# Half of a stage's input turned by a transposing DMA instead of by TensorE, at four places of a two-layer decoder trunk

## The chip, the cores and the metric

One core of a Trainium2 chip runs the whole program. The metric is the time of one execution on the device in microseconds, from the runtime's own start to its end; three runs of a kernel are shown by their median. A profiled execution has its own time, and a span, which goes from its first to its last instruction.

## The reference, cut to what matters

The input `x` has 256 tokens of 1024 numbers, all in fp32. The residual stream `h` runs through two layers; in each it passes three sub-layers (an FFN, a mixer, an FFN), every one with a norm before and behind it. The first layer's mixer is a gated linear recurrence (RG-LRU), the second's is attention on keys and values that are made from the stream between the two layers.

```python
for layer in range(2):
    if layer == 1:
        k, v, c = shared_kv(h, kv_norm_g, w_kv, w_fgate, b_fgate)
    f = swiglu(rms_norm(h, ffn1_pre_g[layer]), ffn1_w_gate[layer], ffn1_w_up[layer], ffn1_w_down[layer])
    h = h + 0.5 * rms_norm(f, ffn1_post_g[layer])
    hn = rms_norm(h, mix_pre_g[layer])
    m = recurrent_block(hn, ...) if layer == 0 else forgetting_attention(hn, ..., k, v, c)
    h = h + rms_norm(m, mix_post_g[layer])
    f = swiglu(rms_norm(h, ffn2_pre_g[layer]), ffn2_w_gate[layer], ffn2_w_up[layer], ffn2_w_down[layer])
    h = h + 0.5 * rms_norm(f, ffn2_post_g[layer])
```

So between the sub-layers `h` is normed and multiplied by the next weight matrix, which needs `h` with the features on the partitions, that is, transposed.

## The kernel before, in words

**Precision by three products.** TensorE multiplies in fp32r, and each fp32 operand is split in an upper part (a copy by ScalarE, called ACT below) and a lower part (the difference, by VectorE, DVE). A product is three matmuls: upper by upper, upper by lower, lower by upper. Weights are split like that as they come: `load_raw` (L161 and L164, a DMA of up to 512 KB on the queue of SP) fills one of five `raw` buffers, `split` makes `whi` (L173, ACT) and `wlo` (L177, DVE), of which there are nine each. One such unit of weights is an item: in most stages two k tiles (128 of the 1024 features each) by 512 columns.

**Two rows of tokens.** `h[0]` and `h[1]` are the tokens 0 to 127 and 128 to 255 (t=0 and t=1). Each item is multiplied first for t=0 and, some slots later, for t=1; `run` lets t=0 go 7 items ahead and then alternates. TensorE (PE) runs in exactly the order in which the program is written. The other engines' order is made by a scheduler at build time, by priorities (`tc.high_priority`) and, where `keep_in_program_order` stands, as written. Once built, each engine runs its own list in order and waits where an operand is not ready. `defer(n, f)` puts work n+1 slots later in the written order.

**From one sub-layer to the next.** `enter(t, ...)` is called when the last product of a sub-layer for row t is written. It takes sums of squares (ACT, into a tile `junk`), makes the scale on GpSimd (POOL) and adds the normed result to `h[t]` in two halves of 512 features (L297, DVE). A few slots later its inner function `inputs` prepares the next stage's operand: `to_tp` (L226) transposes `h[t]` on PE, four 128x128 tiles for each half, into a PSUM bank `gt`; `to_x` then multiplies each half by the gain (`xg`, L234, DVE, which also brings it to SBUF), copies it to the upper part `xhi` (L235, ACT) and takes the lower part `xlo` (L240, DVE). `stat` makes the scale of the norm, which is applied behind the product. At the layer's change there are two targets: `xhi`/`xlo` for the FFN and `zhi`/`zlo` for keys and values, with a gain of its own.

**Tiles that two uses share.** `t1` has two buffers of 512 columns, for products in `enter`, for `xg`, and for the halves in the next point. `junk` has one buffer.

**The other way to transpose, in use already.** The FFN's hidden values, keys, queries of t=1 and gates go another way: `planes` (POOL) parts each fp32 in two 16-bit planes, a transposing DMA on SP's queue turns both (`DMA_TRANSPOSE`, L535 for hidden values, L216 for the others, through `swap`), and `join` (POOL, L540 or L220) puts the halves together again. There are 56 such transfers.

The function `enter` is called for the output of the recurrence (rows go on to the FFN after it), for that of the attention, and for the four FFNs.

Of the kernel before, what the change touches and what calls it, by code (L numbers as in the profile page):

```python
# [9 lines left out]
F32 = mybir.dt.float32  # L10
# [33 lines left out]
def trunk_kernel(ctx: ExitStack, tc: tile.TileContext, A: dict, out: bass.AP):  # L44
# [13 lines left out]
    def nm(s):  # L58
        uid[0] += 1
        return f"{s}_{uid[0]}"  # L60
# [168 lines left out]
    def x_upper(tp, dest, n):  # L229

        gi, xh, xl = dest
        xg = hpool.tile([P, 4, P], F32, tag="t1", name=nm("xg"), bufs=2)
        g = gT[:, gi + 4 * n:gi + 4 * n + 4].unsqueeze(2).to_broadcast([P, 4, P])
        nc.vector.tensor_tensor(xg, tp.rearrange("p (a b) -> p a b", a=4), g, ALU.mult)  # L234
        nc.scalar.activation(xh[:, 4 * n:4 * n + 4, :], xg, AF.Copy)  # L235
        return xg

    def x_lower(xg, dest, n):
        gi, xh, xl = dest
        nc.vector.tensor_tensor(xl[:, 4 * n:4 * n + 4, :], xg, xh[:, 4 * n:4 * n + 4, :].bitcast(F32), ALU.subtract)  # L240

    def to_x(tps, dest):

        with tc.high_priority():
            xg = [x_upper(tps[n], dest, n) for n in range(2)]
            for n in range(2):
                x_lower(xg[n], dest, n)

    def to_x_tiles(tps, dest):

# [15 lines left out]
    def stat(t):  # L266
        ss = new_ss()
        square_sum(h[t], ss[:, 0:1])
        rs[t] = rstd_of(ss, 1)

    def enter(t, dests, pf, gb, half, last=False, normed=False, wait=3):

        f = 1.0 / 16 if half else 1.0 / 32
        ss = new_ss()
        t1 = []
        urgent = tc.high_priority()
        urgent.__enter__()
        for n in range(2):
            square_sum(pf[n], ss[:, n:n + 1], f)
        for n in range(2):  # L280
            if n == 1 and last:
                r = rstd_of(ss, 2, f, nc.vector)
            t1.append(hpool.tile([P, 512], F32, tag="t1", name=nm("t1"), bufs=2))
            nc.vector.tensor_tensor(t1[n], pf[n], gb[:, n * 512:(n + 1) * 512], ALU.mult)
        if not last:
            r = rstd_of(ss, 2, f)

        sp, aq = nc.sync, nc.scalar
        pieces = [(n * 512, 512, None) for n in range(2)]
        if last:  # L290
            pieces = ([(0, 1024, sp)] if t == 0 else
                      [(0, 256, sp), (256, 256, aq), (512, 256, sp), (768, 256, aq)])
        for c, m, q in pieces:
            hn = h[t][:, c:c + m]
            for a in range(c, c + m, 512):
                n = min(m, 512)
                nc.vector.scalar_tensor_tensor(h[t][:, a:a + n], t1[a // 512][:, a % 512:a % 512 + n], r[:, 0:1],  # L297
                                               h[t][:, a:a + n], ALU.mult, ALU.add)
            if last:
                q.dma_start(out[0, t * P:(t + 1) * P, c:c + m], hn)  # L300
        urgent.__exit__(None, None, None)
        if last:
            return

        def inputs():
            tps = [to_tp(h[t], n) for n in range(2)]
            for dest in dests:
                to_x(tps, dest)
            stat(t)

        def norm():
            with tc.high_priority():
                normed_x()

        def normed_x():
            ss = new_ss()
            for n in range(2):
                square_sum(h[t][:, n * 512:(n + 1) * 512], ss[:, n:n + 1])
            rs[t] = rstd_of(ss, 2)
            hn = []  # L320
            for n in range(2):
                hn.append(hpool.tile([P, 512], F32, tag="t1", name=nm("hn"), bufs=2))
                nc.vector.tensor_scalar(hn[n], h[t][:, n * 512:(n + 1) * 512], rs[t][:, 0:1], None, ALU.mult)

            def go():
                tps = []
                for n in range(2):
                    tp = gtbank()
                    for j in range(4):
                        nc.tensor.transpose(tp[:, j * P:(j + 1) * P], hn[n][:, j * P:(j + 1) * P], ident)  # L330
                    tps.append(tp)
                to_x_tiles(tps, dests[0])
            defer(6, go)

        if normed:
            norm()
            settled[0] = True
        else:
            defer(wait, inputs)
# [152 lines left out]
    def ahead(i, fn):  # L492
# [5 lines left out]
            return prep()  # L498
        items[i] = (both, work)

    def ffn_items(pool_of, wg, wu, wd, post_g, next_dests, last=False, normed=False):
        hid = {}
        sil = {}
        box = {}

        def hid_tiles(t):
            if t not in hid:
                hid[t] = (pool_of().tile([P, 22, P], F32R, tag=f"hhi{t}", name=nm("hhi"), bufs=1),
                          pool_of().tile([P, 22, P], F32R, tag=f"hlo{t}", name=nm("hlo"), bufs=1))
            return hid[t]  # L510

        def post_gate(c0, nn):
            def f(t, ps):
                s = pool_of().tile([P, 512], F32, tag="sil", name=nm("sil"), bufs=2)
                nc.scalar.activation(s[:, :nn], ps, AF.Silu, scale=rs[t][:, 0:1])  # L515
                sil[t] = s
            return f

        def post_up(c0, nn):
            def f(t, ps):  # L520
                hh, hl = hid_tiles(t)
                s = sil[t][:, :nn]
                pr = pool_of().tile([P, 512], F32, tag="prod", name=nm("prod"), bufs=2)
                nc.vector.scalar_tensor_tensor(pr[:, :nn], ps, rs[t][:, 0:1], s, ALU.mult, ALU.mult)  # L524
                halves = hpool.tile([P, 512], F32, tag="t1", name=nm("pl"), bufs=2).bitcast(U16)[:, :2 * nn]
                turned = pr.bitcast(U16)[:, :2 * nn].rearrange("p (a b) -> p a b", b=P)
                nc.gpsimd.tensor_copy(halves.rearrange("p (h f) -> p h f", h=2),  # L527
                                      pr[:, :nn].bitcast(U16).rearrange("p (f h) -> p h f", h=2))
                defer(2, lambda: hidden_T(halves, turned, hh, hl))

            def hidden_T(halves, turned, hh, hl):

                m, k0 = nn // P, c0 // P
                keep = tc.keep_in_program_order
                keep(nc.sync.dma_start(turned, halves, transpose=True))  # L535
                hv = hh[:, k0:k0 + m, :].rearrange("p a b -> p (a b)")
                lv = hl[:, k0:k0 + m, :].rearrange("p a b -> p (a b)")

                def join():
                    nc.gpsimd.tensor_copy(halves.rearrange("p (f h) -> p h f", h=2),  # L540
                                          turned.rearrange("p (h a) b -> p h (a b)", h=2))

                def parts():
                    x = halves.bitcast(F32)
                    keep(nc.scalar.activation(hv, x, AF.Copy))  # L545
                    keep(nc.vector.tensor_tensor(lv, x, hv.bitcast(F32), ALU.subtract))  # L546
                defer(3, join)
                defer(7, parts)
            return f

        i0 = len(items)
        for i in range(5):
            proj_items(wg, i * 512, 512, main_x, post_gate(i * 512, 512))
            proj_items(wu, i * 512, 512, main_x, post_up(i * 512, 512))

        last_up = post_up(2560, 256)

        def post_both(t, pg, pu):
            post_gate(2560, 256)(t, pg)
            last_up(t, pu)  # L560

        pair_items(wg, wu, 2560, 256, main_x, post_both)

        def load_gb():
            box["gb"] = gain_bcast(post_g)

        ahead(i0 + 24, load_gb)

        def post_down(t, accs):
            enter(t, next_dests(t), accs, box["gb"], True, last, normed)  # L570

        row_items(wd, [P] * 22, lambda t, k: (hid[t][0][:, k, :], hid[t][1][:, k, :]), post_down, 4 if last else 2)
        return i0

# [644 lines left out]
    def post_q(n):  # L1219
        return lambda t, ps: heads_T(ps, t, n, HD ** -0.5, att["q"][t])  # L1220

    for n in range(2):
        proj_items(A["attn_w_q"][0], n * 512, 512, main_x, post_q(n))
    n_q[0] = len(items)
    row_items(A["attn_w_o"][0], [P] * 8, lambda t, k: (att["oh"][t][:, k, :], att["ol"][t][:, k, :]),
              lambda t, accs: enter(t, [main_dest(GI[("ffn2", 1)], t)], accs, gbox["mix1"], False, wait=4),
              rows0=1, late=True)
    ahead(n_q[0] + 2, load_gb("mix1", A["mix_post_g"][1]))
    n_att = len(items)
# [240 lines left out]
```

## Time and profile before

| | |
|---|---|
| median of 3 runs | 966.11 us (965.6 to 966.61) |
| the profiled execution | 965.92 us |
| its span | 964.2 us |
| PE, PE's weight loads | 955.9 us busy (99%), 791.3 us (82%) |
| DVE, ACT, POOL | 640.7 us (66%), 527.6 us (55%), 218.2 us (23%) |
| granted TensorE clock | 0.999 |
| DMA | 198.79 MB, mean 206 GB/s |

A profile's row in order of time reads: start and duration in us (from the span's start), engine, line of the kernel, operation, what it writes and reads, how many instructions are merged in the row, and in brackets the idle time of the engine before it and what ended that. The chain of work that ended last goes back from the last instruction to what released it, and so on. In a view of one line the three numbers are the shortest, median and longest duration in ns.

### The profile page before, as it was taken

How to read it: one execution, taken by the hardware profiler on the slowest of the kernel's cores; microseconds unless marked ns; L12 is line 12 of the kernel's file. 1: busy time of each engine (PE TensorE's matmuls, PEld its weight loads, DVE VectorE, ACT ScalarE, POOL GpSimd, SP SyncE). 2: the span in 40 equal slices, each digit the busy share in tenths (PEclk: the TensorE clock that was granted, in tenths of full speed). 3: DMA queues.
4: the chain of work that ended last, by engine and by line, in shares of the span. 5: the costliest groups of instructions: out<-in, count | busy, mean ns of one | idle time of the engine just before them, and what ended most of it. 6: DMA issues, size and time to landing. Idle time of an engine off the chain costs nothing.

```text
span 964.2 us, 12866 instructions
## 1 busy us (share of the span) xinstructions
PE 955.9 (99%) x4575; PEld 791.3 (82%) x4575; DVE 640.7 (66%) x845; ACT 527.6 (55%) x750; POOL 218.2 (23%) x221
## 2 busy tenths in 40 slices
PE   9999999999999999999999999999999999999997
PEld 6888888898878888888898888888887788888886
DVE  6658674678997666664686566665488876666642
ACT  7546453568886555443565455444366855444431
POOL 2712330130001323230003522234022012232200
PEclk9999999999999999999999999999999999999999
DMA  8787995475346787775558979878773468777731
GB/s 286 226 258 225 256 284 197 142 228 163 119 123 219 209 236 211 205 242 196 135 182 278 253 219 258 230 216 265 226 256 97 133 199 236 207 222 233 223 109 44
DMA packets 148934, 198.79 MB, mean 206 GB/s; under 512 B 67166, under 2 KB 85958, under 8 KB 148742
## 3 DMA queue, kind: packets, MB, share of 16 engines
q1 hardware_dynamic: 146182, 191.06, 65.6%
q0 software_dynamic: 2080, 6.38, 2.1%
q8 instruction: 36, 0.59, 0.2%
q10 hardware_dynamic: 608, 0.53, 0.2%
q14 instruction: 28, 0.23, 0.1%
HBM read 182.19 MB, written 3.16 MB: 192 GB/s over the span
## 4 chain that ended last, share of the span: by engine, by line
PE 95%; DVE 2%; ACT 1%; issue 1%; POOL 0%; DMA 0%; POOLq 0%; DVEq 0%; ACTq 0%
PE mm L428 16%; PE mm L429 16%; PE mm L432 16%; PE mm L183 13%; PE mm L185 13%; PE mm L184 13%; PE gt L795 2%; PE mm L1305 1%; PE mm L190 1%; PE mm L191 1%; PE mm L192 1%; PE gt L226 1%; ACT pe L1181 1%; DVE wlo L177 0%; PE tr L127 0%
## 5 line engine op out<-in xcount | busy, mean ns | idle before, releaser
L177 DVE TENSOR_TENSOR wlo<-raw,whi 128x1024 fp32r<-128x1024 f32 (+5 forms) x329 | 418.0, 1276 | 230.7 <-ACT whi L173 228.3
L173 ACT ACTIVATE whi<-raw 128x1024 fp32r<-128x1024 f32 (+5 forms) x329 | 341.9, 1045 | 308.6 <-PE mm L432 119.2
L428 PE MATMUL mm<-whi,xhi 128*128 128x512 f32 x656 | 256.6, 391 | 0.0
L429 PE MATMUL mm<-wlo,xhi 128*128 128x512 f32 x656 | 255.5, 389 | 0.0
L432 PE MATMUL mm<-whi,xlo 128*128 128x512 f32 x656 | 202.1, 389 | 0.0
L428 PEld LDWEIGHTS mm<-whi,xhi 128*128 128x128 f32 x656 | 123.2, 188 | 25.9 <-issue 0.7
L432 PEld LDWEIGHTS mm<-whi,xlo 128*128 128x128 f32 x656 | 123.1, 188 | 25.8 <-DVE xlo L240 0.2
L429 PEld LDWEIGHTS mm<-wlo,xhi 128*128 128x128 f32 x656 | 123.2, 188 | 25.4 <-DVE wlo L177 0.3
L183 PE MATMUL mm<-whi,hhi 128*128 128x512 f32 x352 | 137.2, 390 | 0.0
L185 PE MATMUL mm<-whi,hlo 128*128 128x512 f32 x352 | 137.0, 389 | 0.0
L184 PE MATMUL mm<-wlo,hhi 128*128 128x512 f32 x352 | 136.9, 389 | 0.0
L540 POOL COPY pl<-prod 128x1024 uint16<-128x1024 uint16 (+1 forms) x48 | 69.9, 1456 | 174.4 <-DMA prod<-pl 174.4
L527 POOL COPY pl<-prod 128x1024 uint16<-128x1024 uint16 (+1 forms) x48 | 66.3, 1382 | 151.9 <-DVE prod L524 86.8
L183 PEld LDWEIGHTS mm<-whi,hhi 128*128 128x128 f32 x352 | 66.1, 188 | 13.7
L185 PEld LDWEIGHTS mm<-whi,hlo 128*128 128x128 f32 x352 | 66.1, 188 | 13.7
L184 PEld LDWEIGHTS mm<-wlo,hhi 128*128 128x128 f32 x352 | 66.1, 188 | 13.6
L198 POOL TENSOR_SCALAR nv<-ss 128x1 f32<-128x1 f32 x22 | 9.6, 437 | 268.7 <-ACT junk L205 268.7
L524 DVE SCALAR_TENSOR_TENSOR prod<-mm,rstd,sil 128x512 f32<-128x512 f32 (+1 forms) x48 | 33.8, 703 | 29.5 <-PE mm L432 25.9
L515 ACT ACTIVATE sil<-mm,rstd 128x512 f32<-128x512 f32 (+1 forms) x48 | 31.0, 649 | 32.9 <-PE mm L432 25.0
L546 DVE TENSOR_TENSOR hlo<-pl,hhi 128x512 fp32r<-128x512 f32 (+1 forms) x48 | 41.2, 858 | 3.7 <-ACT hhi L545 3.7
L183 PE MATMUL mm<-whi,xhi 128*128 128x512 f32 (+1 forms) x112 | 42.8, 382 | 0.0
L185 PE MATMUL mm<-whi,xlo 128*128 128x512 f32 (+1 forms) x112 | 42.5, 379 | 0.0
(223 smaller groups left out, 1054.6 us busy)
## 6 DMA issues: line engine op xcount, KB each, us to landing
raw<-in_ffn_w_down_dram SPq DMA_DIRECT2D x88, 512.0 KB
raw<-in_ffn_w_up_dram SPq DMA_DIRECT2D x80, 512.0 KB
raw<-in_ffn_w_gate_dram SPq DMA_DIRECT2D x78, 512.0 KB
raw<-in_rg_w_in_dram SPq DMA_DIRECT2D x10, 504.0 KB
raw<-in_rg_w_out_dram SPq DMA_DIRECT2D x10, 504.0 KB
raw<-in_ffn_w_gate_dram SPq DMA_DIRECT2D x19, 256.0 KB
raw<-in_ffn_w_up_dram SPq DMA_DIRECT2D x16, 256.0 KB
raw<-in_rg_w_in_dram SPq DMA_DIRECT2D x8, 512.0 KB
```

The lines of the kernel that those rows point to most:

```text
L173: up = nc.scalar.activation(hi[:parts, c:c + m], rawv[:, c:c + m], AF.Copy)
L177: nc.vector.tensor_tensor(lo[:parts, c:c + m], rawv[:, c:c + m], hi[:parts, c:c + m].bitcast(F32), ALU.subtract)
L183: nc.tensor.matmul(ps, xh, wh, start=first, stop=False)
L184: nc.tensor.matmul(ps, xh, wl, start=False, stop=False)
L185: nc.tensor.matmul(ps, xl, wh, start=False, stop=last)
L428: nc.tensor.matmul(ps, get_x(t, k)[0], u.hi[:, c], start=k == 0, stop=False)
L429: nc.tensor.matmul(ps, get_x(t, k)[0], u.lo[:, c], start=False, stop=False)
L432: nc.tensor.matmul(ps, get_x(t, k)[1], u.hi[:, c], start=False, stop=k == nk - 1)
L524: nc.vector.scalar_tensor_tensor(pr[:, :nn], ps, rs[t][:, 0:1], s, ALU.mult, ALU.mult)
L527: nc.gpsimd.tensor_copy(halves.rearrange("p (h f) -> p h f", h=2), pr[:, :nn].bitcast(U16).rearrange("p (f h) -> p h f", h=2))
L540: nc.gpsimd.tensor_copy(halves.rearrange("p (f h) -> p h f", h=2), turned.rearrange("p (h a) b -> p h (a b)", h=2))
L546: keep(nc.vector.tensor_tensor(lv, x, hv.bitcast(F32), ALU.subtract))
```

## The change

At four places the second half of `inputs` (k tiles 4 to 7) no longer passes PE. These places are t=1 behind the recurrence, t=1 at the layer's change (with both targets), and t=0 and t=1 behind the attention. The other places stay as they were. At a changed place:

- `enter` parts the second half of `h[t]` in planes by POOL as soon as it is there, into a tile `a`;
- `inputs` transposes only the first half on PE (four transposes, one PSUM bank) and issues a transposing DMA of `a` into a tile `b` on SP's queue;
- POOL joins `b` back into `a` one slot later in the written order;
- two slots later (t=0) or four (t=1), `turned_to_x` multiplies `a` by the gain on DVE, copies to `xhi` on ACT and takes `xlo` on DVE; the multiplication and the copy are kept in the written order.

For t=1, `a` is a buffer of `t1` and `b` is the tile `junk`; for t=0 both are halves of the queries of t=0, which are done with by then. At the layer's change the second target's product goes into a buffer of `prod`, which the FFN uses for hidden values.

```diff
     def to_x(tps, dest):
         with tc.high_priority():
-            xg = [x_upper(tps[n], dest, n) for n in range(2)]
-            for n in range(2):
-                x_lower(xg[n], dest, n)
+            xg = [x_upper(tp, dest, n) for n, tp in enumerate(tps)]
+            for n, v in enumerate(xg):
+                x_lower(v, dest, n)
+
+    def turned_to_x(v, dests, more):
+        with tc.high_priority():
+            xs = []
+            for i, (gi, xh, xl) in enumerate(dests):
+                xg = v if i == len(dests) - 1 else more()
+                g = gT[:, gi + 4:gi + 8].unsqueeze(2).to_broadcast([P, 4, P])
+                xs.append(xg.rearrange("p (a b) -> p a b", a=4))
+                tc.keep_in_program_order(
+                    nc.vector.tensor_tensor(xs[i], v.rearrange("p (a b) -> p a b", a=4), g, ALU.mult))
+                tc.keep_in_program_order(nc.scalar.activation(xh[:, 4:, :], xs[i], AF.Copy))
+            for xg, dest in zip(xs, dests):
+                x_lower(xg, dest, 1)
...
-    def enter(t, dests, pf, gb, half, last=False, normed=False, wait=3):
+    def enter(t, dests, pf, gb, half, last=False, normed=False, wait=3, spare=None):
...
+        by_transfer = (spare or t == 1) and not (half and (len(dests) == 1 or t == 0)) and not normed
+        if by_transfer:
+            a = spare() if t == 0 else hpool.tile([P, 512], F32, tag="t1", name=nm("hp"), bufs=2)
+            with tc.high_priority():
+                planes(a.bitcast(U16), h[t][:, 512:])
+
         def inputs():
-            tps = [to_tp(h[t], n) for n in range(2)]
+            tps = [to_tp(h[t], n) for n in range(1 if by_transfer else 2)]
             for dest in dests:
                 to_x(tps, dest)
             stat(t)
+            if by_transfer:
+                b = spare() if t == 0 else spool.tile([P, 512], F32, tag="junk", name=nm("ht"), bufs=1)
+                with tc.high_priority():
+                    swap(b.bitcast(U16), a.bitcast(U16))
+                defer(0, lambda: join(a.bitcast(U16).rearrange("p (f h) -> p h f", h=2), b.bitcast(U16)))
+                defer(1 + 2 * t, lambda: turned_to_x(a, dests, spare))
...
+    def old_products():
+        return pools["f"].tile([P, 512], F32, tag="prod", name=nm("hp"), bufs=2)
...
-            enter(t, next_dests(t), accs, box["gb"], True, last, normed)
+            enter(t, next_dests(t), accs, box["gb"], True, last, normed, spare=old_products)
...
+    q_parts = [1, 0]
+
+    def old_q():
+        return att["q"][0].rearrange("p a b -> p (a b)").rearrange("p (s f) -> p s f", s=2)[:, q_parts.pop(), :]
...
-              lambda t, accs: enter(t, [main_dest(GI[("ffn2", 1)], t)], accs, gbox["mix1"], False, wait=4),
+              lambda t, accs: enter(t, [main_dest(GI[("ffn2", 1)], t)], accs, gbox["mix1"], False, wait=4,
+                                    spare=old_q),
```

What this does to the engines' lists is shown at the layer's change, for t=1 (the lines of the changed kernel have moved: L428 is L454 there, L1099 is L1128). First PE, before: `h_75` is `h[1]`, `gt` the PSUM banks, `mm` the running product of t=0.

```order
L432 MATMUL mm_4398<-whi_4270,xlo 128x512 x2
L226 MATMUL gt_4417<-ident,h_75 128x128 x4
L226 MATMUL gt_4422<-ident,h_75 128x128 x4
L428 MATMUL mm_4398<-whi_4282,xhi 128x512
L429 MATMUL mm_4398<-wlo_4283,xhi 128x512
L428 MATMUL mm_4398<-whi_4282,xhi 128x512
L429 MATMUL mm_4398<-wlo_4283,xhi 128x512
```

And PE in the changed kernel:

```order
L458 MATMUL mm_4399<-whi_4269,xlo 128x512 x2
L226 MATMUL gt_4418<-ident,h_75 128x128 x4
L454 MATMUL mm_4399<-whi_4281,xhi 128x512
L455 MATMUL mm_4399<-wlo_4282,xhi 128x512
L454 MATMUL mm_4399<-whi_4281,xhi 128x512
L455 MATMUL mm_4399<-wlo_4282,xhi 128x512
```

One group of four transposes is gone, and the product that followed the second group follows the first. PE's list has the same difference at the other three places, and no other in the whole program. Next SP's queue in the changed kernel, at the same place (`raw` is a load of weights, `gb` of a gain):

```order
L1128 DMA raw_4528<-in_w_kv_dram 128x2x340
L369 DMA gb_5264<-in_ffn_post_g_dram 128x1024
L1128 DMA raw_4547<-in_w_kv_dram 128x2x340
L216 DMA_TRANSPOSE ht_4438<-hp_4391 128x8x128
L1128 DMA raw_4561<-in_w_kv_dram 128x2x340
L1128 DMA raw_4580<-in_w_kv_dram 128x2x340
```

The transposing transfer stands behind the first load of weights that follows the gain; without it the list is that of before. Last DVE, from the residual's second half on, before:

```order
L297 SCALAR_TENSOR_TENSOR h_75<-t_842_4384,rstd_4388,h_75 128x512
L177 TENSOR_TENSOR wlo_4355<-raw_4351,whi_4354 128x720
L234 TENSOR_TENSOR xg_4427<-gt_4417,gT 128x512
L234 TENSOR_TENSOR xg_4430<-gt_4422,gT 128x512
L177 TENSOR_TENSOR wlo_4362<-raw_4358,whi_4361 128x720
L240 TENSOR_TENSOR xlo<-xg_4427,xhi 128x4x128
L240 TENSOR_TENSOR xlo<-xg_4430,xhi 128x4x128
L234 TENSOR_TENSOR xg_4435<-gt_4417,gT 128x512
L234 TENSOR_TENSOR xg_4438<-gt_4422,gT 128x512
L177 TENSOR_TENSOR wlo_4395<-raw_4392,whi_4394 128x680
L240 TENSOR_TENSOR zlo_4246<-xg_4435,zhi_4245 128x4x128
L240 TENSOR_TENSOR zlo_4246<-xg_4438,zhi_4245 128x4x128
```

And DVE in the changed kernel (`hp` are the tiles of the turned half; L258 is the multiplication by the gain in `turned_to_x`, `z_4494` the forget gate's first step):

```order
L177 TENSOR_TENSOR wlo_4361<-raw_4357,whi_4360 128x720
L240 TENSOR_TENSOR xlo<-xg_4423,xhi 128x4x128
L177 TENSOR_TENSOR wlo_4396<-raw_4393,whi_4395 128x680
L234 TENSOR_TENSOR xg_4427<-gt_4418,gT 128x512
L240 TENSOR_TENSOR zlo_4245<-xg_4427,zhi_4244 128x4x128
L258 TENSOR_TENSOR hp_4468<-hp_4391,gT 128x512
L258 TENSOR_TENSOR hp_4391<-hp_4391,gT 128x512
L240 TENSOR_TENSOR xlo<-hp_4468,xhi 128x4x128
L1080 SCALAR_TENSOR_TENSOR z_4494<-mm_4449,rstd_4322,bfb 128x16
L177 TENSOR_TENSOR wlo_4485<-raw_4482,whi_4484 128x680
L240 TENSOR_TENSOR zlo_4245<-hp_4391,zhi_4244 128x4x128
```

DVE has as many instructions as before; the two products for the second half now read the joined tile, and the next split of weights (`wlo_4485`) stands behind them. ACT's list changes in the same way: the copies to `xhi` and `zhi` for the second half move down, and one split of weights stands behind the first of them.

## The prediction

> **What bounds the kernel now.** I read the page's first lines first.
>
> ```profile
> PE 955.9 (99%) x4575; PEld 791.3 (82%) x4575; DVE 640.7 (66%) x845; ACT 527.6 (55%) x750; POOL 218.2 (23%) x221
> ...
> PE 95%; DVE 2%; ACT 1%; issue 1%; POOL 0%; DMA 0%; POOLq 0%; DVEq 0%; ACTq 0%
> ```
>
> PE is busy for 955.9 of 964.2 us and makes 95% of the chain that ended last. Busy time alone would not say that PE is never starved, since its spans overlap, so I asked next for whom PE's matmuls wait.
>
> ```profile
> PE tr L127 <- PEq L1455: 0.8, 1, 0.8
> PE gt L795 <- issue: 0.8, 1, 0.8
> PE gt L1165 <- POOL qT L220: 0.3, 1, 0.3
> ```
>
> The columns are the total, the number of times and the longest, in us. That is the whole list: 1.9 us in the program, none at the four changed places. So whatever leaves PE's list leaves the time, as long as PE finds its operands as punctually as now. That is the whole question here: a small sure gain against four new chains of work that must not be late.
>
> **What goes.** Sixteen transposes, four at each place. The chain in order of time has the eight of each place as one piece (start, us, what):
>
> ```profile
> 304.52 0.87 PE gt L226 x8
> ...
> 485.84 0.87 PE gt L226 x8
> ...
> 771.37 0.88 PE gt L226 x8
> ...
> 783.14 0.87 PE gt L226 x8
> ```
>
> Eight cost 0.87 us (0.88 once), so four cost 0.435, and four places 4 x 0.435 = **1.74 us**. Removing them shortens no wait, since none was there. That the half that stays costs half is an assumption; the other reading of the price is the third rival.
>
> **What comes, at each place.** A chain takes the transposes' place: POOL parts the half (`planes`), a transposing DMA turns it, POOL joins it, DVE multiplies, ACT copies to `xhi`. DVE and ACT have the same number of instructions as before, only later. The same chain is run for the queries of t=1, and there it can be read (POOL and SP in order of time):
>
> ```profile
> 730.78 1.90 POOL L212 COPY pl<-htok 128x1024 uint16<-128x1024 uint16 x1 [14.64 <-DVE htok L1015]
> 735.82 1.69 POOL L220 COPY qT<-htok 128x1024 uint16<-128x1024 uint16 x1 [3.14 <-DMA htok<-pl]
> 741.25 1.04 POOL L212 COPY pl<-htok 128x1024 uint16<-128x1024 uint16 x1 [3.75 <-DVE mx L1179]
> 745.41 1.35 POOL L220 COPY qT<-htok 128x1024 uint16<-128x1024 uint16 x1 [3.12 <-DMA htok<-pl]
> 732.70 1.24 SPq L216 DMA_TRANSPOSE htok<-pl  x1
> 195.57 4.31 SPq L161 DMA_DIRECT2D raw<-in_rg_w_in_dram  x3
> 200.39 1.26 SPq L216 DMA_TRANSPOSE turned<-pl  x1
> 205.93 2.07 POOL L220 COPY tokT<-turned 128x1024 uint16<-128x1024 uint16 x1 [2.48 <-DMA turned<-pl]
> L234 DVE TENSOR_TENSOR xg<-gt,gT x20: 680/683/692, 298.0 to 784.2; 128x512 f32<-128x512 f32 x20
> L235 ACT ACTIVATE xhi<-xg x16: 614/632/636, 298.7 to 785.6; 128x512 fp32r<-128x512 f32 x16
> ```
>
> Parting takes 1.04 to 1.90 us, I take the middle, 1.47. From a transfer's issue to the join's start it is 735.82 - 732.70 = 3.12 us on a quiet queue, and 205.93 - 200.39 = 5.54 where three loads of weights went out just before. At the changed places one or two loads stand shortly ahead in SP's list, so I take 4.0, about a third of the way. The join takes 1.35 to 2.07; I take 1.52, the mean of the two joins of queries. Then 0.68 on DVE and 0.63 on ACT, and some 0.2 for two handings over between engines (the square sum on ACT below starts 0.1 behind the residual it reads). Together: 0.2 + 1.47 + 4.0 + 1.52 + 0.68 + 0.63 = **8.5 us** from the residual's second half to `xhi`; at the ends of all rows 7.0 and 11.0.
>
> **The tightest place, the layer's change.** Rows of DVE, ACT, SP and PE:
>
> ```profile
> 484.44 1.40 DVE L297 SCALAR_TENSOR_TENSOR h<-t,rstd,h 128x512 f32<-128x512 f32 x2
> 493.25 0.87 DVE L177 TENSOR_TENSOR wlo<-raw,whi 128x680 fp32r<-128x680 f32 x1 [0.19 <-ACT whi L173]
> 485.94 1.06 ACT L205 ACTIVATE junk<-h 128x1024 bf16<-128x1024 f32 x1 [1.54 <-DVE h L297]
> 492.45 0.77 ACT L173 ACTIVATE whi<-raw 128x680 fp32r<-128x680 f32 x1 [0.70 <-PE mm L432]
> 486.74 0.37 SPq L1099 DMA_DIRECT2D raw<-in_w_kv_dram  x1
> 495.53 0.39 PE L428 MATMUL mm<-whi,xhi 128*128 128x512 f32 x1
> 498.41 0.32 PE L184 MATMUL mm<-wlo,zhi 128*128 128x340 f32 x1
> L428 PEld LDWEIGHTS mm<-whi,xhi x656: 186/188/191, 19.0 to 890.2; 128*128 128x128 f32 x164
> ```
>
> The residual is there at 484.44 + 1.40 = 485.84. SP is free at 486.74 + 0.37 = 487.1 and the tile `junk` at 487.0, both before the planes are (485.84 + 0.1 + 1.47 = 487.4), so the planes set the issue. `xhi` is ready at 485.84 + 8.5 = 494.3 (492.8 to 496.8). PE first reads k tile 4 of t=1 in the third item of that row, by its list the matmul at 495.53; the load of that operand starts 0.19 ahead, and everything comes 0.44 earlier now: 494.9. So the middle has **0.6 us to spare**, the early end 2.1, and the late end is 1.9 late.
>
> Here DVE and ACT wait too. DVE stands before its first product until 493.0; then its second, `xlo` (behind `xhi`: 494.3 + 0.68 = 495.0), a small step of the forget gate and the split of weights (0.87) end at about 496.0. The matmul that reads this split is the one at 498.41, so it must be there at 498.41 - 0.63 = 497.8: 1.8 to spare. That ACT's split of 492.45 was released by PE, and not by a DMA, says that loads are ahead of the need; SP's 1.24 us of issue is paid from that.
>
> **The other places.**
>
> ```profile
> 303.10 1.42 DVE L297 SCALAR_TENSOR_TENSOR h<-t,rstd,h 128x512 f32<-128x512 f32 x2 [0.31 <-POOL rstd L200]
> 313.34 1.23 DVE L177 TENSOR_TENSOR wlo<-raw,whi 128x1024 fp32r<-128x1024 f32 x1 [4.15 <-ACT whi L173]
> 316.13 0.39 PE L428 MATMUL mm<-whi,xhi 128*128 128x512 f32 x1
> 765.01 1.42 DVE L297 SCALAR_TENSOR_TENSOR h<-t,rstd,h 128x512 f32<-128x512 f32 x2 [0.25 <-POOL rstd L200]
> 780.25 0.39 PE L428 MATMUL mm<-whi,xhi 128*128 128x512 f32 x1
> 779.82 1.42 DVE L297 SCALAR_TENSOR_TENSOR h<-t,rstd,h 128x512 f32<-128x512 f32 x2 [0.24 <-POOL rstd L200]
> 793.40 0.39 PE L428 MATMUL mm<-whi,xhi 128*128 128x512 f32 x1
> ```
>
> Residual plus 8.5 against PE's need (the matmul on k tile 4, less 0.63): behind the recurrence 313.0 against 315.5; behind the attention 774.9 against 779.6 for t=0 and 789.7 against 792.8 for t=1. That is 2.5, 4.7 and 3.1 us to spare; with 11.0 instead of 8.5 it is 0.0, 2.2 and 0.6. Behind the recurrence DVE's new wait lies in the 4.15 us in which it stood idle anyway. The buffer of `t1` that holds the half comes free with `xlo`; its next user, the planes of a hidden half, reads a product that stands behind `xlo` in DVE's list anyway. So three places hide the chain even at its late end, and one hides it in the middle.
>
> **A rule that speaks against the change.** These rows of DVE and POOL bear on the eight copies that POOL gets (about 12 us on an engine that is 23% busy):
>
> ```profile
> 798.05 1.68 DVE L177 TENSOR_TENSOR wlo<-raw,whi 128x1024 fp32r<-128x1024 f32 x1 [0.77 <-ACT whi L173]
> 797.36 1.35 POOL L540 COPY pl<-prod 128x1024 uint16<-128x1024 uint16 x1 [3.69 <-DMA prod<-pl]
> ```
>
> A split of weights takes 1.23 us alone (the row of 313.34 above), and this one took 1.68, where a copy of POOL ran until 798.71. The Trainium skill (SBUF — State Buffer, section Who interferes with whom) says that a VectorE instruction with two SBUF inputs and a GpSimd one that reads SBUF lock each other out for the whole instruction. By that rule the trace agrees: 798.05 + 1.68 - 798.71 = 1.02 us is left for the split itself; and planes that meet the split at the layer's change would be held until it ends, which the 1.90 above includes. The sum is the same by both; with 1.90 for 1.47 the 0.6 us there shrinks to 0.2.
>
> **The rivals.**
>
> *The turned half is late at the layer's change.* PE waits there for up to 1.9 us: 964.4 to 966.3, with 0.9 as its middle 965.3. For it: the small margin, and that it depends on a transfer's backlog. Against it: the middle allows 4.0 us for a transfer of which the quiet row shows 3.12.
>
> *Slower: the transfer stands behind a backlog.* One transfer in the trace does:
>
> ```profile
> 578.73 1.14 POOL L988 DMA_DIRECT2D bias1d<-crows  x1
> 578.81 1.24 SPq L535 DMA_TRANSPOSE prod<-pl  x1
> 589.99 2.20 POOL L540 COPY pl<-prod 128x1024 uint16<-128x1024 uint16 x1 [10.13 <-DMA prod<-pl]
> ```
>
> From issue to join 11.18 us. At the layer's change that gives `xhi` at 485.84 + 8.5 + 11.18 - 4.0 = 501.5, PE 6.6 us late, DVE and ACT held as long, and a time of 966.11 - 1.74 + 6.6 = **971.0**. It decides from 4.0 + 0.6 + 1.74 = 6.3 us on. Against it: POOL's queue had issued a bulk transfer (the attention's bias, the first row) just ahead of that one, and no such transfer stands in the lists at the changed places. The Trainium skill (VectorE: DVE Perf Modes, section Rules for kernel authors) sides with this rival: it wants a 128x128 transpose on TensorE where PSUM will do as its target. No wait of PE in this trace decides on that rule, and the rows above (0.435 us against 8.5) agree with it for latency alone.
>
> *Faster: a transpose costs its duration.* The view of that line has
>
> ```profile
> L226 PE MATMUL gt<-ident,h x64: 270/272/274, 296.5 to 783.7; 128*128 128x128 f32 x64
> ```
>
> With 0.272 us each, sixteen would be 4.35 us, and the time 961.8. Against it: the chain's 0.87 for eight, where durations overlap.
>
> That the change leaves PE's work as it is, is excluded by PE's list.
>
> **How the numbers follow.** Against the profiled execution the sum is 965.92 - 1.74 = 964.18; that execution lies 0.19 below the median, so for the median 966.11 - 1.74 = **964.4**. Chances: hidden everywhere 0.62; late at the layer's change 0.23; slower by the backlog 0.09; faster by the full durations 0.06. A measurement of this kernel tells about 0.2%, 1.9 us, from no change, that is 964.18 and 968.04. The forecast lies 0.2 us inside that line and the runs before spread by 0.5 each way, so a third of its chance (0.21) counts as faster: 0.27 with the last rival. Slower is 0.09, the rest 0.64. The range takes in the forecast less the 0.5 of the runs, and the late end of the first rival plus a little: 963.8 to 966.5. It leaves out the two last rivals and the tails.
>
> **What would show it.** In the changed kernel's profile: the pieces of L226 at the four places at 0.43 us instead of 0.87; PE's list of waits without a new row on L454 or L458 from ACT or DVE; the join behind L216 starting 3 to 5 us after the transfer's issue; DVE's L258 at the layer's change starting before 493.4 on the old clock. A wait of PE's loads of `xhi` there would show the first rival, one over 1.74 us the second. I am wrong in kind if PE waits at another of the places, or if splits of weights come late behind the held DVE.

## The result, and the profile after

The changed kernel takes **964.78 us** (median of 22 runs, 964.31 to 965.18), the kernel before beside it 965.88 (22 runs, 965.41 to 967.97). The ratio is 0.9987, with a 95% interval from 0.9981 to 0.9992: 1.25 us less, 0.77 to 1.83. Ratios leave disturbed runs out, so they can differ a little from the quotient of two medians. The profiled execution took 965.18 us, its span is 963.5, and the granted clock 0.999.

The page's first line, and PE's whole list of waits (total, times, longest, in us):

```profile
PE 954.8 (99%) x4559; PEld 789.6 (82%) x4559; DVE 646.0 (67%) x845; ACT 527.5 (55%) x750; POOL 236.5 (25%) x229
```

```profile
PE gt L824 <- issue: 0.8, 1, 0.8
PE tr L127 <- PEq L1490: 0.8, 1, 0.8
PE gt L1194 <- POOL qT L220: 0.2, 1, 0.2
PE mm L1237 <- ACT pT L1225: 0.2, 1, 0.2
```

There are 16 matmuls less (4575 before), and no row says that a product waits for `xhi` or `xlo` (it would stand at L454 or L458). POOL has its eight copies more, 18 us (the prediction had about 12). So the chains are hidden at all four places. The chain in order of time has the pieces of transposes at half their length, and the last matmul is from PE's rows in order of time:

```profile
305.05 0.44 PE gt L226 x4
...
485.97 0.44 PE gt L226 x4
...
771.22 0.44 PE gt L226 x4
...
782.57 0.44 PE gt L226 x4
```

```profile
956.73 0.39 PE L185 MATMUL mm<-whi,hlo 128*128 128x512 f32 x1
```

Set against the kernel before (304.52, 485.84, 771.37, 783.14 for the pieces, and 957.73 for that last matmul) these starts lie at +0.53, +0.13, -0.15, -0.57 and -1.00 us. Each step down is one place: -0.40, -0.28, -0.42, -0.43, together -1.53. The interval of 0.77 to 1.83 us still holds the forecast gain of 1.74; that the gain is smaller is read from these rows. The +0.53 was there before the first place, from the program's first matmuls on; whether that belongs to the change is asked below. So is the end: from the last matmul to the end of the span it is 6.8 us now (963.5 - 956.73) and was 6.5 (964.2 - 957.73).

The tightest place, the layer's change, in rows of DVE, POOL, SP, ACT and PE in order of time:

```profile
484.57 1.41 DVE L311 SCALAR_TENSOR_TENSOR h<-t,rstd,h 128x512 f32<-128x512 f32 x2
485.90 0.90 DVE L177 TENSOR_TENSOR wlo<-raw,whi 128x720 fp32r<-128x720 f32 x1
486.05 1.65 POOL L212 COPY hp<-h 128x1024 uint16<-128x1024 uint16 x1 [1.77 <-DVE h L311]
487.72 1.24 SPq L216 DMA_TRANSPOSE ht<-hp  x1
491.79 1.35 POOL L220 COPY hp<-ht 128x1024 uint16<-128x1024 uint16 x1 [2.31 <-DMA ht<-hp]
493.17 1.42 DVE L258 TENSOR_TENSOR hp<-hp,gT 128x512 f32<-128x512 f32 x2 [1.34 <-POOL hp L220]
493.90 0.63 ACT L259 ACTIVATE xhi<-hp 128x512 fp32r<-128x512 f32 x1 [2.79 <-DVE hp L258]
495.29 0.39 PE L454 MATMUL mm<-whi,xhi 128*128 128x512 f32 x1
```

The residual was there at 485.98 (484.57 + 1.41). `xhi` was ready at 494.53, 8.55 us later, and the matmul that reads it stood at 495.29, its operand load 0.19 ahead: 0.57 us to spare. The transfer took 4.07 us from issue to join.

### The profile page after: what moved, and what is told of

Its sections match the earlier page's. It is cut to its first block, busy times and chain, and to the rows that moved or that the text cites. A ratio compares the mean times of both kernels' runs of the same rounds, so it can differ in the third digit from the quotient of the medians.

```text
span 963.5 us, 12847 instructions
## 1 busy us (share of the span) xinstructions
PE 954.8 (99%) x4559; PEld 789.6 (82%) x4559; DVE 646.0 (67%) x845; ACT 527.5 (55%) x750; POOL 236.5 (25%) x229
## 4 chain that ended last, share of the span: by engine, by line
PE 95%; DVE 2%; ACT 1%; issue 1%; POOL 0%; DMA 0%; POOLq 0%; DVEq 0%; ACTq 0%
PE mm L454 16%; PE mm L455 16%; PE mm L458 16%; PE mm L183 13%; PE mm L185 13%; PE mm L184 13%; PE gt L824 2%; PE mm L1340 1%; PE mm L190 1%; PE mm L191 1%; PE mm L192 1%; ACT pe L1210 1%; PE gt L226 1%; PE tr L127 0%; DVE wlo L177 0%
## 5 line engine op out<-in xcount | busy, mean ns | idle before, releaser
L177 DVE TENSOR_TENSOR wlo<-raw,whi 128x1024 fp32r<-128x1024 f32 (+5 forms) x329 | 423.0, 1293 | 213.9 <-ACT whi L173 212.4
L454 PE MATMUL mm<-whi,xhi 128*128 128x512 f32 x656 | 256.7, 391 | 0.0
L455 PE MATMUL mm<-wlo,xhi 128*128 128x512 f32 x656 | 255.5, 389 | 0.0
L458 PE MATMUL mm<-whi,xlo 128*128 128x512 f32 x656 | 202.2, 389 | 0.0
L454 PEld LDWEIGHTS mm<-whi,xhi 128*128 128x128 f32 x656 | 123.2, 188 | 25.9 <-issue 0.7
L458 PEld LDWEIGHTS mm<-whi,xlo 128*128 128x128 f32 x656 | 123.1, 188 | 26.0 <-DVE xlo L240 0.2
L455 PEld LDWEIGHTS mm<-wlo,xhi 128*128 128x128 f32 x656 | 123.2, 188 | 25.3 <-DVE wlo L177 0.3
L198 POOL TENSOR_SCALAR nv<-ss 128x1 f32<-128x1 f32 x22 | 11.4, 517 | 252.8 <-ACT junk L205 252.8
```

Source lines behind the costliest of these rows:

```text
L177: nc.vector.tensor_tensor(lo[:parts, c:c + m], rawv[:, c:c + m], hi[:parts, c:c + m].bitcast(F32), ALU.subtract)
L454: nc.tensor.matmul(ps, get_x(t, k)[0], u.hi[:, c], start=k == 0, stop=False)
L455: nc.tensor.matmul(ps, get_x(t, k)[0], u.lo[:, c], start=False, stop=False)
L458: nc.tensor.matmul(ps, get_x(t, k)[1], u.hi[:, c], start=False, stop=k == nk - 1)
```

## The experiments

Theory A is the prediction's: the gain is the pitch of sixteen transposes, the chains cost nothing while they stay hidden, and what differs at the start is spread between executions. Theory B: the chains cost something as well, which eats part of 1.74. Beside these stand the prediction's rivals on the price of a transpose and on a late or backed-up transfer.

### The changed kernel again, and without chains

The first is the changed kernel as it is:

> The changed kernel once more, as the measure for the three beside it. Theory A (the gain is the 1.74 us of the sixteen transposes, the chains cost nothing): 1.2 to 1.8 us below the kernel before, PE's list of waits without a row of xhi or xlo. Theory B (the chains cost about 0.5 us somewhere, so the gain is some 1.2): the same total, but with a loss that shows in every execution at one place, at the start or in the attention. What only one execution shows (the first matmuls 0.5 us later than in the execution before, the end 0.3 later) is spread by theory A and would be here again by theory B.

In the second, the condition only drops the transposes:

```diff
-        by_transfer = (spare or t == 1) and ...
+        fewer = (spare or t == 1) and ...
+        by_transfer = False
...
-            tps = [to_tp(h[t], n) for n in range(1 if by_transfer else 2)]
+            tps = [to_tp(h[t], 0)] * 2 if fewer else [to_tp(h[t], n) for n in range(2)]
```

> The sixteen transposes are gone and no chain takes their place: k tiles 4 to 7 at the four places are filled from the first half's transposes a second time, by DVE and ACT as in the kernel before (so this part of the input is not the residual's second half). It gives the price of sixteen transposes alone. Theory A: 1.74 us below the kernel before and within 0.3 us of the changed kernel. Theory B: still 1.74 below the kernel before, the changed kernel 0.5 above it. A transpose that costs its 0.272 us: 4.35 us below the kernel before.

Measured beside each other, the kernel before at 965.81: the changed kernel 964.56 us, ratio 0.9988 (0.9979 to 0.9997); without chains **964.55**, ratio 0.9991 (0.9982 to 1.0000). So the medians show no cost of the chains, with an interval of some 0.9 us each way, and the sixteen transposes alone are worth about what the change is worth. That the two medians agree to 0.01 us is partly luck: by the profiles the kernel without chains gains 0.1 us more on PE (below) and ends 0.3 us sooner (next section), and three of its eleven runs took 966.2 to 966.4. Where the rest of the 1.74 is, the pieces of the chain in order of time say, of the changed kernel's new execution and of the one without chains:

```profile
304.38 0.44 PE gt L226 x4
...
485.30 0.44 PE gt L226 x4
...
770.60 0.44 PE gt L226 x4
...
781.95 0.44 PE gt L226 x4
```

```profile
304.69 0.44 PE gt L226 x4
...
485.61 0.44 PE gt L226 x4
...
770.80 0.44 PE gt L226 x4
...
782.15 0.44 PE gt L226 x4
```

With the last matmul at 956.11 and 956.31, the steps are -0.40, -0.23, -0.42, -0.43 (sum -1.48) and -0.40, -0.34, -0.42, -0.43 (sum -1.59). The start lies at -0.14 and +0.17 now where it was +0.53: spread. The second step is short in all of them. Compared matmul by matmul it is -0.43 at the layer's change itself; 0.08 comes back just behind it, with and without chains, and no run shows why. Up to 0.12 more comes back in the attention in the changed kernel's profiles. The chains need not cost that: the version with four idle loads (next section) has the chains, and its steps sum to -1.60.

### The end of the program

> The kernel before against itself: a ratio of 1.000, and a second profile of it. If the 0.5 us at the start of the one execution and 0.2 the other way of the next are spread of the start (theory A), this profile's first matmuls lie off the first profile's by a few tenths as well, and from 10 us to the end its distance to that one does not change by more than 0.1; the changed kernel's changes by 0.39 to 0.43 at each of the four places, 1.63 to 1.65 in all.

It took 966.04 us against 966.00, ratio 1.0000 (0.9991 to 1.0009). Its transposes start at 304.54 and its last matmul stands at 957.73, 0.02 and 0.00 from the first profile, where I had expected the start to differ by a few tenths. That the start is spread thus rests on the changed kernel's three profiles: +0.53, -0.14 and, in the last one below, -0.36. From the last matmul to the end of the span it is 6.5 us here and without chains (962.8 - 956.31), but 6.74 to 6.75 in the changed kernel's three executions. That contradicts my expectation that the longer end was spread. SP's waits in the last microseconds, of the kernel before, of the changed kernel, and of the one without chains (1.4, 1.7, 1.4 us for the outputs' DMAs):

```profile
SPq L1465 <- DMA out_dram<-h: 1.4, 4, 0.5
```

```profile
SPq L1500 <- DMA out_dram<-h: 1.7, 4, 0.6
```

```profile
SPq L1501 <- DMA out_dram<-h: 1.4, 4, 0.5
```

At the program's end SP looks at the semaphores of the DMAs one after the other, 0.06 us each. DMAs are counted on eight of them in turn, and four more transfers shift the turn by four, so that four looks that used to pass while the outputs were under way now stand behind the last landing: in the trace of the changed kernel four of them do, in that of the kernel before none, and 4 x 0.06 = 0.24 us. If that is the longer end, four idle loads bring the old turn back:

```diff
         keep(nc.gpsimd.memset(kv["one"], 1.0))
+        for t in kv["spare"]:
+            nc.sync.dma_start(t, A["b_fgate"].partition_broadcast(P))
```

> The changed kernel with four loads of 8 KB more on SP's queue, between the recurrence and the second layer, of data that nobody reads. It asks about the end of the program. From PE's last matmul to the end of the span it took 6.48 to 6.49 us in both profiles of the kernel before and in the one without chains, and 6.74 to 6.75 in all three of the changed kernel. The completions of the DMAs are counted on eight semaphores in turn, and the change issues four DMAs more, so the last output is counted on another one than before; at the end SP looks at them one after the other, and after the last output's landing it still has four to look at, at 0.06 us each, that it had behind it before. Four loads more bring the turn round to where it was: the end at 6.48 us again, and the time 0.26 below the changed kernel (964.3 to 964.5 beside a kernel before of 965.9), if that is it. If the longer end comes from the chains or from chance: 6.74 as before, and no gain.

Measured: **964.22 us** (kernel before 965.81), ratio 0.9983 (0.9974 to 0.9992), and the last row reads as before the change:

```profile
SPq L1503 <- DMA out_dram<-h: 1.3, 4, 0.5
```

The end is 6.5 us again (6.48, as before the change), and the time is 1.59 below the kernel before. The mechanism stands by the profile; the 0.3 to 0.6 us against the changed kernel's medians are too little for the intervals alone to prove, but seven of the eleven runs lie below 964.29, the lowest of the changed kernel's 44. This version has the lowest median of those run. So theory A holds for PE, and theory B for the program's end: four transfers more cost 0.26 us there.

### What a transpose costs

```diff
             tps = [to_tp(h[t], n) for n in range(1 if by_transfer else 2)]
+            if by_transfer:
+                unused = to_tp(h[t], 1)
+                for j in range(8):
+                    nc.tensor.transpose(unused[...], h[t][:, 512 + j % 4 * P:...], ident)
```

> The chains of the changed kernel, and PE transposes the second half all the same, three times over, into a bank that nobody reads: 48 transposes more than in the changed kernel. At the pitch of 0.109 us: 5.2 us above the changed kernel, 3.5 above the kernel before. At the duration of 0.272 us: 13.1 above the changed kernel. If the chains were what decides at these places (theory B in a strong form), PE would have time to spare there and the 48 would cost less than 5.2, by as much as PE waits now.

Measured 969.75 us, ratio 1.0042 (1.0029 to 1.0054): 5.19 above the changed kernel, 0.108 for each of 48. The pieces of the first place:

```profile
304.36 0.87 PE gt L226 x8
305.23 0.88 PE gt L330 x8
```

The view of L226 has 0.272 us for one here too, so the duration is not the price; the pitch is. And the 48 cost their whole pitch, so PE had no idle time at these places that they could have filled.

### The spare time at the layer's change

POOL does its join there twice, three and four times, which as written lengthens that chain and nothing else:

```diff
-                defer(0, lambda: join(...))
+                defer(0, lambda: [join(...) for _ in range(2 if len(dests) == 2 else 1)])
```

(3 and 4 for the other two). But DVE's list was laid out anew by the scheduler: in each, a split of weights moved ahead of `xlo`.

> The join at the layer's change twice instead of once: a chain 1.35 us longer. Spare time of 0.57 us: PE waits 0.8 us, the time is 0.8 above the changed kernel (965.3) and still below the kernel before by 0.3 to 0.5. If the loss of 6.4 us with three extra joins is a matter of the held DVE and ACT in general, it is more than 1.5 above the changed kernel already here.

Measured 965.72 us, ratio 0.9997 (0.9989 to 1.0006): no gain that the interval shows, and 0.9 to 1.2 above the changed kernel's medians, where 0.8 was forecast. The rows of PE:

```profile
495.36 0.50 PE L454 MATMUL mm<-whi,xhi 128*128 128x512 f32 x1 [0.45 <-ACT xhi L259]
...
496.16 0.39 PE L455 MATMUL mm<-wlo,xhi 128*128 128x512 f32 x1
496.67 0.50 PE L458 MATMUL mm<-whi,xlo 128*128 128x512 f32 x1
```

`xhi` was late: PE's rows ahead of the place lie 0.55 us before those of the changed kernel's first profile, and this matmul lies 0.07 behind (495.36 against 495.29), 0.62 in all. The chain took 9.87 us from the residual to `xhi`, 1.32 more than 8.55. So 1.32 - 0.62 = 0.70 us were to spare by this run, where the trace of the changed kernel gives 0.57: it is small, as the prediction had it. Behind the moved split `xlo` came late by another 0.3 (it follows L455 by 0.51 instead of 0.22).

> The join there three times: two more, of 1.35 to 1.87 us as the rows with three extra ones have it, so 2.7 to 3.3 us more chain and a wait of PE of 2.1 to 2.7 us. In the run with three extra joins PE waited 3.8 us and then ran eight matmuls at half the clock (granted 0.50 to 0.54 from 498.7 to 501.5), which cost 1.9 us more. If a wait of 2.1 to 2.7 us leaves the clock alone: 2.1 to 2.7 above the changed kernel (966.7 to 967.3). If the clock falls behind any wait of some microseconds: 4 or more above it.

Measured 968.83 us, ratio 1.0023 (1.0012 to 1.0033). Its seven runs fall in two groups: 966.87, 966.92, 967.07, and then 968.83 to 969.83. The profiled one took 969.83; PE's wait there, and the stretches of time behind it (PE, PEld, DVE, ACT and POOL busy, granted clock, DMA share, GB/s):

```profile
PE mm L454 <- ACT xhi L259: 3.1, 1, 3.1
```

```profile
498.00:499.50 1.50, 1.47 (x6) 1.24 (x7) 1.22 (x4) 1.50 (x5) 0.00 (x0) 1.00 0.00 0
499.50:501.00 1.50, 1.50 (x5) 1.19 (x4) 1.47 (x6) 1.00 (x2) 0.00 (x0) 0.51 0.04 11
501.00:502.50 1.50, 1.50 (x5) 1.21 (x5) 1.36 (x6) 0.21 (x1) 0.00 (x0) 0.50 0.18 30
```

After a wait of 3.1 us the clock was granted at half for some 3 us, which costs another 1.5 to 2. The two groups lie about that far apart, and the mean granted clock that is on record for each run parts them in the same way: 0.999 in the three short runs, 0.996 and 0.997 in the four long ones. So it fell in four of seven. Of the wait of 3.1 us, 0.7 is the transfer's: it took 4.76 us in this execution instead of 4.07.

> At the layer's change alone POOL does its join four times instead of once, so the chain is longer by 3 x 1.35 = 4.05 us and nothing else is. Theory A with the spare time read from the trace (0.57 us): PE waits 3.5 us there and all of it stays in the time, 3.5 above the changed kernel and 2.0 to 2.3 above the kernel before. If the spare is larger than read, or the delay is made up later: under 2 above the changed kernel. If the held DVE and ACT make the weights late as well: more than 4 above it.

Measured 970.93 us (970.17 to 972.54), ratio 1.0058 (1.0044 to 1.0072), 6.4 above the changed kernel instead of 3.5. PE's wait, and the stretches:

```profile
PE mm L454 <- ACT xhi L259: 3.8, 1, 3.8
```

```profile
498.50:500.00 1.50, 1.28 (x3) 1.09 (x4) 1.50 (x4) 0.80 (x2) 0.00 (x0) 0.54 0.00 0
500.00:501.50 1.50, 1.50 (x5) 1.07 (x5) 1.40 (x6) 0.00 (x0) 0.00 (x0) 0.50 0.15 40
501.50:503.00 1.50, 1.50 (x7) 1.22 (x6) 0.74 (x3) 0.77 (x1) 0.00 (x0) 0.82 0.57 203
```

The wait is what A expected (3.5, here 3.8). PE is 5.7 us later behind the place in this execution, and of the 1.9 beyond the wait 1.7 are the half clock: the three stretches make 1.4 + 1.5 + 0.5 = 3.4 us of it. The Trainium skill (TensorE: Matmul & The Clock Gate, section Part 1: The HAM clock gate) says that the clock goes to half after an idle window of about 3.4 us, and that the windows run free of the program. By that rule the trace agrees at 0.45 us of waiting (no drop) and at 3.8 (a drop, of 3.4 us). The drop behind 3.1 us does not follow from it, since 3.1 us hold no whole window; there the measurement decides.

### A fifth place, behind a bulk transfer

```diff
-        by_transfer = (spare or t == 1) and not (half and (len(dests) == 1 or t == 0)) and not normed
+        by_transfer = (spare or t == 1) and not (half and t == 0) and not normed
```

> A fifth place gets the chain: t=1 behind the first FFN of the second layer, four transposes less (0.43 us). There POOL's queue has issued a bulk transfer of the attention's bias 1.4 us before the residual is ready, which lands 10.3 us after it. The chain: planes until 714.9, issue there, and PE reads k tile 4 of t=1 at 725.7. If a transfer behind a bulk transfer of POOL takes 11.2 us as the one at 578.81 did (the rival of the prediction), xhi is there at about 728.9 and PE waits 3 to 3.6 us: 2.6 to 3.2 above the changed kernel, and by another 1 to 2 if the clock falls too. If the bulk transfer does not hold it (4 to 5.5 us as at the four places): all hidden, 0.4 below the changed kernel (964.1).

Measured 973.26 us, ratio 1.0079 (1.0065 to 1.0092): 8.7 above the changed kernel's 964.56. POOL and SP in order of time, then PE's wait:

```profile
714.28 0.63 POOL L1038 DMA_DIRECT2D bias<-bias1d  x1
...
725.76 1.31 POOL L220 COPY hp<-ht 128x1024 uint16<-128x1024 uint16 x1 [10.27 <-DMA ht<-hp]
...
714.36 1.24 SPq L216 DMA_TRANSPOSE ht<-hp  x1
```

```profile
PE tr L1057 <- DVE htok L1044: 5.4, 1, 5.4
```

From issue to join 11.40 us: the prediction's second rival, at a place where its condition holds. The price is higher than I had put on it (5.2 above the changed kernel at most, with the clock), by two things. DVE stands before L258 for 9.7 us with the attention's steps behind it in its list, so PE misses not `xhi` but `htok`, earlier. And the granted clock stays at 0.50, in the stretches of time behind the wait:

```profile
729.00:732.00 3.00, 1.88 (x7) 1.69 (x8) 2.37 (x16) 1.55 (x8) 0.00 (x0) 0.50 0.01 3
732.00:735.00 3.00, 3.00 (x11) 2.41 (x10) 1.68 (x4) 3.00 (x13) 0.00 (x0) 0.50 0.00 0
```

Then the bulk transfer behind the join:

```diff
-        tc.keep_in_program_order(nc.gpsimd.dma_start(att["bias1"], kv["bias1"]))
+        defer(6, lambda: tc.keep_in_program_order(nc.gpsimd.dma_start(att["bias1"], kv["bias1"])))
```

> The fifth place again (t=1 behind the first FFN of the second layer), and POOL issues the bulk transfer of the attention's bias behind that place's join instead of ahead of its transfer; its first reader stands at 738.5 us, so it has some 8 us beyond the 10 to 12 that it takes. If the bulk transfer was what held the turned half by 11.3 us: issue to join 4 to 5.5 us, no wait of PE there, the step of the fifth place -0.42 and the time 0.4 below the changed kernel of the same call. If the place itself is too tight: a wait of PE stays, and the time is above the changed kernel.

Measured 966.82 us, ratio 1.0007 (0.9998 to 1.0016), against 964.62 for the changed kernel beside it. The profiled execution is a long one (968.81; its first matmuls lie 1.1 us behind those of the changed kernel's first profile), so only distances within it are used. POOL, SP and DVE in order of time:

```profile
716.11 1.24 SPq L216 DMA_TRANSPOSE ht<-hp  x1
721.59 1.34 POOL L220 COPY hp<-ht 128x1024 uint16<-128x1024 uint16 x1 [3.70 <-DMA ht<-hp]
722.97 0.69 DVE L258 TENSOR_TENSOR hp<-hp,gT 128x512 f32<-128x512 f32 x1 [3.81 <-POOL hp L220]
...
724.97 0.28 DVE L1203 CUSTOM_DVE_ANT_0 pe<-gt,bias 128x128 f32<-128x128 f32 x1
```

The transfer is back at 5.48 us, so the bulk transfer was what held it; `xhi` is in time, and the place itself gains its 0.42. The forecast of 0.4 below is wrong all the same. DVE waits 3.8 us for the join, and the attention's first reduction (L1203), behind it in the list, starts 10.92 us after the residual (712.64 + 1.41 = 714.05 by L311), where the changed kernel has 8.52 (721.44 - 712.92). PE loses 2.6 us in the attention. From the last matmul to the end it is 7.1 us (967.1 - 959.99), 0.4 more than in the changed kernel, which the turn of the semaphores does not explain. Together that is -0.4 + 2.6 + 0.4 = 2.6, and 2.2 was measured. A chain that is hidden from PE held an engine that PE waits for a little later.

> As the run with five places and the bulk transfer behind, and a sixth place, t=0 behind the same FFN (planes and turned half in the two product buffers). There the residual is ready at 702.3 and PE's need is some 9.4 us later, against chains of 8.6 to 9.7 us as the four places had them: between 0.8 to spare and 0.3 late. Hidden: 0.8 to 0.9 below the changed kernel of the same call. Late by up to 0.3: 0.5 to 0.6 below.

The edit lets t=0 through as well (`not (half and t == 0 and len(dests) == 2)`). Measured 968.97 us, ratio 1.0028 (1.0017 to 1.0038), 4.35 above the changed kernel, where 0.5 to 0.9 below it was forecast. At the sixth place PE gains 0.42, then waits for the other row's residual. DVE and POOL there:

```profile
701.74 3.19 DVE L177 TENSOR_TENSOR wlo<-raw,whi 128x1024 fp32r<-128x1024 f32 x2
...
707.19 2.31 DVE L177 TENSOR_TENSOR wlo<-raw,whi 128x1024 fp32r<-128x1024 f32 x1
```

```profile
701.89 1.97 POOL L212 COPY hp<-h 128x1024 uint16<-128x1024 uint16 x1 [1.51 <-DVE h L311]
...
706.98 1.51 POOL L220 COPY hp<-hp 128x1024 uint16<-128x1024 uint16 x1 [1.31 <-DMA hp<-hp]
```

The split at 707.19 takes 2.31 us instead of 1.21; the join it meets ends at 708.49, and 1.01 us are left to it after that. The two splits at 701.74 take 3.19 instead of 2.35 beside the planes. That is 1.9 us of DVE where DVE has no idle time, and the second row's residual comes some 2 us late.

```profile
PE gt L226 <- DVE h L311: 0.9, 1, 0.9
```

By PE's rows 1.7 us are lost here, 0.9 gained at the two places, and 3.0 lost in the attention, as with five places: the larger part of the 4.35 is again the held DVE there.

> The changed kernel beside the two: 964.5 to 964.8 us, 1.1 to 1.3 below the kernel before.

Measured 964.62 us, ratio 0.9983 (0.9974 to 0.9992), as expected.

## Why the prediction was right

- **What bounds the kernel, and what goes.** Right. PE's list sets the time, and on PE dropping transposes from it is what the change brings: without chains the time is the same within the interval, and 48 transposes put back cost their whole pitch. The size was a little high. At the places themselves four are worth 0.40 to 0.44 where I took 0.435, and 0.1 to 0.2 in all comes back behind the layer's change and in the attention: 1.48 to 1.60 in place of 1.74.
- **A step that was missing.** The 0.26 us at the end of the program. I counted POOL's copies, SP's issues and every wait, but not that the number of DMAs decides which output SP looks at last. 1.48 to 1.60 less 0.26 gives 1.22 to 1.34, and 1.25 was measured; with the old turn it was 1.59. The kernel without chains, which does not pay the 0.26, fits less well: 1.59 by its steps, 1.26 by its medians, with an interval that takes in both. The forecast of 964.4 is off by 0.2 to 0.4 only, and not by the 0.5 that the gain lacks, since the kernel before came out at 965.8 to 966.0 in the later runs and not at 966.11. That part is luck.
- **The chain.** 8.5 us came out 8.55 at the layer's change, with planes longer than I had them (1.65 for 1.47) and a join that was shorter (1.35 for 1.52): two errors that cancel. At the other three the planes took 1.90 to 1.97. The Trainium skill's rule on VectorE and GpSimd (SBUF — State Buffer, section Who interferes with whom) has planes beside a split held until it ends. By that rule the trace agrees to 0.2 us: at the layer's change a split ends at 486.80 (485.90 + 0.90) and the planes at 487.70 (486.05 + 1.65), 0.90 later, and planes alone take 1.04. Behind the recurrence and at t=1 behind the attention the whole chain took 9.7 us, and 11.2 at t=0, where DVE's and ACT's lists held its last steps; the spare times there, 1.3, 1.0 and 2.0 us, were about half or less of the 2.5, 3.1 and 4.7 that I had.
- **The tightest place.** Right: 0.6 to spare by forecast, 0.57 by the trace, 0.70 by the kernel with one join more, which lost 0.6 at `xhi` and 0.3 at `xlo`. The 4.0 us for the transfer were a guess between two rows. Here it took 3.8 to 4.2 us in ten profiled executions and 4.76 in one, which would have left the changed kernel nothing; at the two other places behind a load it mostly took 4.9 to 5.6.
- **The rivals.** A late half did not come; the backlog did not come at the four places. Where a bulk transfer stands ahead it came at 11.40 us, and cost 8.8 us of PE at that place, more than the 6.6 that I had for the layer's change: a wait of 5.4, and behind it the lowered clock, which the sum left out. The third rival is refuted by the 48 transposes.

## What to carry to other kernels

On the engine that sets the end, an instruction is worth its pitch in the stream and not its duration, and the work that replaces it costs that engine next to nothing as long as it is in time: compare the chain with the reader's place row by row, and look at every engine that the chain makes wait, since what stands behind it in that engine's list may be needed sooner than the operand. A wait of PE of 3 us or more can cost half as much again by the clock (here at 3.1 us in four of seven runs, and at 3.8 and 5.4), so a late chain turns a gain of 0.4 us into a loss of several. When a gain is a fraction of a microsecond, compare the program's start and end apart from its middle, over several executions.

## What the runs showed of the hardware that I had not expected

- Behind a wait of 3.1 to 3.8 us the granted clock was 0.50 to 0.54 for about 3 us, with matmuls of 0.63 instead of 0.39 us; behind 5.4 us it was 0.50 for 6.
- The same kernel with a wait of about 3.1 us gave two times some 2 us apart (966.9 to 967.1 at a mean granted clock of 0.999, and 968.8 to 969.8 at 0.996 to 0.997).
- SP's looks at the DMAs' semaphores at the end of the program cost 0.26 us more with four DMAs more in the program, and nothing more with eight.
- A split of weights that meets a copy of POOL took up to 2.31 us in place of 1.21, about the copy's rest (1.30) and then its own time (1.01 of it left).
- A transposing transfer took 3.1 us on a quiet queue, 3.8 to 5.6 behind one load issued about 0.85 us earlier, and 11.4 behind a bulk transfer of POOL issued 0.08 us earlier.
